# A two-layer decoder trunk on one core: layer 1's output product as seven half-size block products, with the block sums of its weight made during attention

## The chip, the core and the metric

One core of a Trainium2 chip runs the whole program. The metric is device time in microseconds (us) of one execution; of several executions the median counts. PE is the engine of the matrix products (PEld its weight loads), DVE the vector engine, ACT the scalar engine, POOL the GpSimd engine; SP only issues DMA transfers here, and ACT issues some too.

## What is computed

The reference has two layers over a sequence of 1024 rows of width 1024, all float32. Layer 0 (a recurrence and a gated spatial mix) is the same before and after. Layer 1 is sliding-window attention with a gate, then one output product:

```python
def swa_mixer(h, w_in, sinks, w_out):          # layer 1
    p = h @ w_in                               # q (16 heads of 64), k, v (2 heads each), z
    ...                                        # banded softmax, window 128, ALiBi, sinks
    y = out.reshape(bsz, t_len, ODD_MIX) * jax.nn.silu(z)
    return y @ w_out                           # 1024x1024 times 1024x1024

for i in range(DEPTH):
    ...
    x = x + gate * y                           # gate: one row of 1024, the same for every row of x
return rmsnorm(x, final_g)                     # per row: x / sqrt(mean(x*x) + eps) * final_g
```

## The kernel before

A float32 product is made of three passes of a faster format: each operand is split into `hi` (a copy that ACT rounds) and `lo` (the raw value less `hi`, by DVE, named `V` in the code, or POOL, named `G`), and `mm` on line 118 is called for hi·hi, hi·lo and lo·hi into the same PSUM tile. So every weight block passes through a tile `wraw` (three buffers, loaded by the SP queue), an ACT copy and a subtraction before PE can use it.

Layer 1 works on the transposed stream. The head pair n (two heads of 64) takes part n of w_in: `head_projs(n)` makes the queries (`qproj`) and the gate path (`zgate`, into `y`) for both halves of the sequence, 512 rows each. `attend(n, half, ...)` (lines 1187 to 1241) then goes over four blocks of 128 queries. For each: scores on PE into `pS`; DVE adds the bias (L1207); ACT takes the exponential (L1211); DVE the reciprocal (L1213); POOL scales each head's scores `Sx` (L1215); PE transposes them into `pT` (L1221); ACT and DVE split that (L1226, L1227); PE multiplies with the values into `po`. For each pair of blocks ACT and DVE add the two accumulators into `cm` (L1236 to L1239), and POOL multiplies `y` by it (L1241). `y` is then the transposed left operand of the output product, [128, 8, 1024].

Order: within layer 1 a scheduler sets the order of each engine from the program text, the dependences and priorities; `attend` stands at a raised priority. Each engine and each DMA queue takes its instructions in that order, one by one. For the head pairs 4 to 7 (N1 = 4) the second half's `attend` is written after the loop and after the loads of the output weight, so its work is mixed with that of the first output rows.

The output weight `owo` is loaded in 16 pieces of 128x512 through `wraw` (lines 1292 to 1301), split by ACT (L1299) and by DVE and POOL in turn (L1300). Then, for each of eight blocks of 128 rows (L1321 to L1354): `y` is split into `yh` (ACT, L1325) and `yl` (DVE, 128x1024, L1326); for each half of 512 columns PE makes 24 matmuls (8 blocks of the inner dimension, 3 passes) into a PSUM tile `op`; DVE multiplies it by `gate` (L1338) and adds it to the residual `xr` (L1339); ACT takes the sum of squares (L1340); DVE and POOL make the scale of the row (L1344 to L1346); DVE scales both halves (L1349); two DMAs store them. The last block is cut into columns of 512, 256 and 256, so that less is left after the last matmul. The weight is not multiplied by the gate; each product is.

Of the kernel before, what the change touches and what calls it, by code (L numbers as in the profile page):

```python
# [93 lines left out]
def tile_kernel(ctx, tc, x, cons, par, rows, ada, ada0, ew, wup, sgw, sgb, ewo, ow, owo, out, dbg=None):  # L94
# [1057 lines left out]
    at = ctx.enter_context(tc.tile_pool(name="at", bufs=1, side="right", reuse_waits="tile"))  # L1152
# [32 lines left out]
    N1 = 4  # L1185
# [64 lines left out]
    def qproj(n, w, half):  # L1250
        pt = proj(w, h, half)
        Q = []
        for e in range(2):
            a = slice(e * 64, e * 64 + 64)
            o = slice(64 - e * 64, 128 - e * 64)
            tag, bufs = ("QL", 2 * (KC - N1)) if half and n >= N1 else ("Q", 8)
            q = at.tile([P, HT], F32R, name="Q", tag=tag, bufs=bufs)
            S.activation(q[a, :], pt[a, :], AF.Copy, scale=-0.125)
            V.scalar_tensor_tensor(out=q[o, :], in0=pt[a, :], scalar=-0.125, in1=q[a, :].bitcast(F32), op0=ALU.mult, op1=ALU.subtract)
            Q.append(q)  # L1260
        qs[n, half] = Q

    def head_projs(n):
        wq = wload(ow[n])
        if n < KC - 1:
            for half in range(2):
                qproj(n, wq, half)
        wz = wload(ow[10 + n])
        for half in range(2):
            if n == KC - 1:  # L1270
                qproj(n, wq, half)
            zgate(n, wz, half)
# [9 lines left out]

    qs = {}
    head_projs(0)
    for n in range(KC):
        bias = biases(n)
        for half in range(2 if n < N1 else 1):
            with tc.high_priority(offset=BOOST):
                attend(n, half, qs[n, half], bias)
        if n + 1 < KC:  # L1290
            head_projs(n + 1)

    wo = []
    for n in range(2):
        hi, lo = new_hh(n)
        for k in range(KC):
            raw = wp.tile([P, HT], F32, name="wraw", tag="wraw", bufs=3)
            nc.sync.dma_start(out=raw, in_=owo[k * P:(k + 1) * P, n * HT:(n + 1) * HT])
            S.activation(hi[:, k, :], raw, AF.Copy)  # L1299
            (V if k % 2 else G).tensor_tensor(out=lo[:, k, :], in0=raw, in1=hi[:, k, :].bitcast(F32), op=ALU.subtract)  # L1300
        wo.append((hi, lo))
    for n in range(N1, KC):
        with tc.high_priority(offset=BOOST):
            attend(n, 1, qs[n, 1], biases(n))
    if "y1" in dbg:
        for j in range(8):
            nc.sync.dma_start(out=dbg["y1"][j], in_=y[:, j, :])


    def half_tiles(name, tag, bufs, src, dt=F32):  # L1310
        ts = [at.tile([P, HT], dt, name=name, tag=tag, bufs=bufs) for n in range(2)]
        for n in range(2):
            nc.scalar.dma_start(out=ts[n], in_=src(slice(n * HT, (n + 1) * HT)))
        return ts

    gate = half_tiles("gate", "Q", 8, lambda ns: gated[1, ns].partition_broadcast(P))
    gb = half_tiles("gateb", "zth", 2, lambda ns: rows[1, ns].partition_broadcast(P))
    for n in range(2):
        V.tensor_tensor(out=gate[n], in0=gate[n], in1=gb[n], op=ALU.add)
    fg = half_tiles("fg", "zth", 2, lambda ns: rows[2, ns].partition_broadcast(P))  # L1320
    for b in range(NB):  # L1321
        sl = slice(b * P, (b + 1) * P)
        yh = wp.tile([P, KC, P], F32R, name="yh", tag="whi", bufs=2)
        yl = wp.tile([P, KC, P], F32R, name="yl", tag="wlo", bufs=2)
        S.activation(yh, y[:, :, sl], AF.Copy)  # L1325
        V.tensor_tensor(out=yl, in0=y[:, :, sl], in1=yh.bitcast(F32), op=ALU.subtract)  # L1326
        xt = half_tiles("xr", "Q", 8, lambda ns: x1d[sl, ns])
        st = at.tile([P, 4], F32, name="st", tag="st", bufs=4)
        cuts = (0, HT, D) if b < NB - 1 else (0, HT, HT + 256, D)
        for i, (c0, c1) in enumerate(zip(cuts, cuts[1:])):  # L1330
            wh, wl = (w[:, :, c0 % HT:c0 % HT + c1 - c0] for w in wo[c0 // HT])
            xs_ = xt[c0 // HT][:, c0 % HT:c0 % HT + c1 - c0]
            pt = pproj("op")[:, 0:c1 - c0]
            for k in range(KC):
                mm(pt, lhsT=yh[:, k, :], rhs=wh[:, k, :], start=(k == 0), stop=False)
                mm(pt, lhsT=yh[:, k, :], rhs=wl[:, k, :], start=False, stop=False)
                mm(pt, lhsT=yl[:, k, :], rhs=wh[:, k, :], start=False, stop=(k == KC - 1))
            V.tensor_tensor(out=pt, in0=pt, in1=gate[c0 // HT][:, c0 % HT:c0 % HT + c1 - c0], op=ALU.mult)  # L1338
            V.tensor_tensor(out=xs_, in0=pt, in1=xs_, op=ALU.add)  # L1339
            S.activation(pt, xs_, AF.Square, accum_out=st[:, i:i + 1])  # L1340
            if b == NB - 1:
                (V if c1 == D else G).tensor_tensor(out=xs_, in0=xs_, in1=fg[c0 // HT][:, c0 % HT:c0 % HT + c1 - c0], op=ALU.mult)
        for i in range(1, len(cuts) - 1):
            V.tensor_tensor(out=st[:, 0:1], in0=st[:, 0:1], in1=st[:, i:i + 1], op=ALU.add)  # L1344
        V.tensor_scalar(out=st[:, 0:1], in0=st[:, 0:1], scalar1=1.0 / D, scalar2=NORM_EPS, op0=ALU.mult, op1=ALU.add)
        G.tensor_tensor(out=st[:, 3:4], in0=st[:, 0:1], in1=nhalf[:, 0:1], op=ALU.pow)  # L1346
        for n in range(2):
            if b < NB - 1:
# [61 lines left out]
```

## Time and profile before

| what | value |
|---|---|
| time, median of 3 runs | 1119.16 us (1118.9 to 1120.5) |
| the profiled execution: its own time, and its span in the trace | 1120.78 us, 1119.0 us |
| mean granted clock of PE, as a share of full speed | 0.976 |
| busy share of the span: PE, DVE, ACT, POOL | 93%, 64%, 47%, 34% |
| matmuls in the program | 7912 |
| layer 1's attention, roughly | from 745 us, its last pieces at 1067 us |
| output product on PE | from 1003 us on, alone from about 1050 to 1112 us |

The span is the time from the first to the last instruction of the trace; it is a little shorter than the execution's own time. A row of a timeline gives the start in us, the duration in us, the engine, the line in the kernel, the operation, and `result<-operands` with its shape; in brackets stands how long the engine sat idle before it and what ended that.

### The profile page before, as it was taken

How to read it: one execution, taken by the hardware profiler on the slowest of the kernel's cores; microseconds unless marked ns; L12 is line 12 of the kernel's file. 1: busy time of each engine (PE TensorE's matmuls, PEld its weight loads, DVE VectorE, ACT ScalarE, POOL GpSimd, SP SyncE). 2: the span in 40 equal slices, each digit the busy share in tenths (PEclk: the TensorE clock that was granted, in tenths of full speed). 3: DMA queues.
4: the chain of work that ended last, by engine and by line, in shares of the span. 5: the costliest groups of instructions: out<-in, count | busy, mean ns of one | idle time of the engine just before them, and what ended most of it. 6: DMA issues, size and time to landing. Idle time of an engine off the chain costs nothing. (4 is left out here: it accounts for less than half of the span.)

```text
span 1119.0 us, 20771 instructions
## 1 busy us (share of the span) xinstructions
PE 1038.8 (93%) x7912; PEld 833.5 (74%) x7912; DVE 716.3 (64%) x1666; ACT 526.6 (47%) x1252; POOL 382.5 (34%) x474
## 2 busy tenths in 40 slices
PE   3899898999898898989998999999999999999997
PEld 2677676677676676676776788878888888878886
DVE  6865858585749576777545367764655644478754
ACT  5575435554344436553332132234665654487521
POOL 3642405131215123233335100043554543467201
PEclk8799999999989999998999999999999999999999
DMA  8710212122202321133334244321100111152121
GB/s 306 267 26 20 78 57 67 31 67 67 76 13 68 101 66 60 39 104 105 124 118 149 90 135 134 121 71 48 39 27 31 39 39 38 52 181 67 70 95 56
DMA packets 55131, 93.42 MB, mean 83 GB/s; under 512 B 5748, under 2 KB 15988, under 8 KB 55032
## 3 DMA queue, kind: packets, MB, share of 16 engines
q1 hardware_dynamic: 45032, 77.10, 21.4%
q10 hardware_dynamic: 10000, 15.01, 4.1%
q8 instruction: 62, 1.02, 0.4%
q14 instruction: 37, 0.30, 0.1%
HBM read 79.49 MB, written 12.59 MB: 82 GB/s over the span
## 5 line engine op out<-in xcount | busy, mean ns | idle before, releaser
L118 PE MATMUL pproj<-hi,wlo 128*128 128x512 f32 x704 | 285.0, 405 | 2.4 <-POOL wlo L246 2.4
L118 PE MATMUL pproj<-hi,whi 128*128 128x512 f32 x704 | 284.7, 404 | 0.8 <-ACT vt L1175 0.7
L118 PE MATMUL pproj<-lo,whi 128*128 128x512 f32 x704 | 285.0, 405 | 0.0
L246 POOL TENSOR_TENSOR wlo<-wraw,whi 128x512 fp32r<-128x512 f32 x86 | 115.9, 1368 | 170.2 <-ACT whi L245 169.4
L118 PEld LDWEIGHTS pproj<-hi,whi 128*128 128x128 f32 x704 | 133.8, 190 | 28.8 <-issue 2.1
L118 PEld LDWEIGHTS pproj<-hi,wlo 128*128 128x128 f32 x704 | 133.4, 189 | 28.3 <-POOL wlo L246 3.3
L118 PEld LDWEIGHTS pproj<-lo,whi 128*128 128x128 f32 x704 | 133.9, 190 | 25.5 <-issue 0.5
L245 ACT ACTIVATE whi<-wraw 128x512 fp32r<-128x512 f32 x102 | 59.0, 623 | 76.8 <-PE htp L122 31.6
L118 PE MATMUL op<-wo,whi 128*128 128x512 f32 x256 | 80.8, 396 | 1.1 <-ACT whi L245 1.1
L1211 ACT ACTIVATE Sx<-Sx,nm 128x257 f32<-128x257 f32 (+1 forms) x128 | 62.3, 489 | 27.7 <-DVE nm L1207 25.8
L1207 DVE CUSTOM_DVE_ANT_0 Sx<-pS,bias,nsink 128x256 f32<-128x256 f32 (+1 forms) x128 | 53.5, 464 | 30.2 <-PE pS L118 28.9
L1215 POOL TENSOR_SCALAR Sx<-Sx,rc 128x256 f32<-128x256 f32 (+1 forms) x128 | 60.5, 487 | 26.3 <-DVE rc L1213 23.8
L842 DVE SCALAR_TENSOR_TENSOR adacc<-araw,cond,adacc 128x512 f32<-128x512 f32 x56 | 48.7, 869 | 27.5 <-DMA araw<-ada 27.3
L1227 DVE TENSOR_TENSOR PL<-pT,PH 128x512 fp32r<-128x512 f32 (+1 forms) x64 | 41.7, 655 | 30.2 <-ACT PH L1226 29.6
L118 PEld LDWEIGHTS op<-wo,whi 128*128 128x128 f32 x256 | 48.0, 188 | 12.9 <-ACT whi L245 1.5
L118 PE MATMUL op<-hi,yl 128*128 128x512 f32 (+1 forms) x136 | 51.8, 381 | 0.4 <-DVE yl L1326 0.4
L118 PE MATMUL op<-hi,yh 128*128 128x512 f32 (+1 forms) x136 | 51.7, 380 | 0.4 <-ACT yh L1325 0.4
L118 PE MATMUL op<-lo,yh 128*128 128x512 f32 (+1 forms) x136 | 51.6, 379 | 0.0
L118 PE MATMUL op<-wo,wlo 128*128 128x512 f32 x128 | 51.3, 400 | 0.0
L645 DVE TENSOR_TENSOR pr<-Lf,LT 128x2 f32<-128x2 f32 (+14 forms) x120 | 45.2, 376 | 2.6
L213 POOL TENSOR_TENSOR st<-st,nhalf 128x1 f32<-128x1 f32 x16 | 10.4, 650 | 98.8 <-DVE st L212 98.8
L1226 ACT ACTIVATE PH<-pT 128x512 fp32r<-128x512 f32 (+1 forms) x64 | 35.7, 563 | 17.8 <-PE pT L1221 16.4
(310 smaller groups left out, 2151.2 us busy)
## 6 DMA issues: line engine op xcount, KB each, us to landing
araw<-ada SPq DMA_DIRECT2D x64, 256.0 KB, 2.7
wraw<-ew SPq DMA_DIRECT2D x50, 256.0 KB, 3.0
wraw<-ow SPq DMA_DIRECT2D x36, 256.0 KB, 2.9
adaraw<-ada SPq DMA_DIRECT2D x16, 512.0 KB, 5.8
x<-x SPq DMA_DIRECT2D x8, 512.0 KB, 6.2
woraw<-ewo SPq DMA_DIRECT2D x16, 256.0 KB, 3.1
xr<-x ACTq DMA_DIRECT2D x16, 256.0 KB, 3.1
wraw<-y0d SPq DMA_DIRECT2D x16, 256.0 KB, 4.5
```

Of the source, the lines that this page charges most:

```text
L118: last[0] = nc.tensor.matmul(out, lhsT=lhsT, rhs=rhs, **kw).ins
L213: G.tensor_tensor(out=st[:, 3:4], in0=st[:, 2:3], in1=nhalf[:, 0:1], op=ALU.pow)
L245: a = S.activation(hi[:, gs, :], raws[g], AF.Copy)
L246: b = E.tensor_tensor(out=lo[:, gs, :], in0=raws[g], in1=hi[:, gs, :].bitcast(F32), op=ALU.subtract)
L645: V.tensor_tensor(out=pr[:, 0:nc_, 0:i + 1], in0=Lf[:, i:i + 1, 0:i + 1].to_broadcast([P, nc_, i + 1]), in1=LTt[:, 0:nc_, 0:i + 1], op=ALU ...
L842: op = V.scalar_tensor_tensor(out=acc, in0=raw, scalar=cond[:, k:k + 1], in1=acc, op0=ALU.mult, op1=ALU.add)
L1207: V.tensor_tensor_reduce(out=Sx[:, e, off:2 * P], in0=pS3[:, e, 0:nk], in1=bias[e][:, off:], scale=1.0, scalar=nsink[:, hd:hd + 1], op0=AL ...
L1211: S.activation(pr[:, e, off:2 * P + 1], Sx[:, e, off:2 * P + 1], AF.Exp, bias=nm[:, e:e + 1], scale=-1.0, accum_out=sm[:, e:e + 1])
L1215: G.tensor_scalar(out=pr[:, e, off:2 * P], in0=pr[:, e, off:2 * P], scalar1=rc[:, e:e + 1], scalar2=0.5, op0=ALU.mult, op1=ALU.mult)
L1226: S.activation(PH[:, ks, :], pT2[:, ks, :], AF.Copy)
L1227: V.tensor_tensor(out=PL[:, ks, :], in0=pT2[:, ks, :], in1=PH[:, ks, :].bitcast(F32), op=ALU.subtract)
```

## The change

Left operand y and weight W are each seen as 2x2 blocks of 512x512 (y's rows by its inner dimension, W's inner dimension by its columns). Eight block products make the output before; now seven do, with Winograd's form of Strassen's scheme. With B the gated weight, the seven right operands are B11, B21, B22, T1 = B12 − B11, T3 = B22 − B12, T2 = T3 + B11 and T4 = B21 − T2; the left ones are blocks of y or sums of them (`s3`, `s1`, `s2`, `s4`).

1. The gate is folded into the weight: `load_gate` (after the first head pair) makes two gate tiles, and `make_ops(k)` (after head pairs 1 to 4, one k of four each) loads four pieces of 128x512, multiplies each by the gate and makes the four sums, all on POOL: eight operations of 128x512 for each k. The seven results are written by SP to a DRAM scratch `wgd`.
2. `load_op` reads an operand back through `wraw` in four pieces and splits it (ACT, then DVE or POOL). B11 comes after head pair 5, the others during the output product.
3. No attention is held back: `attend` runs for both halves of every head pair within the loop, and the queries of the next pair are made before the gate path of this one.
4. The output product runs as B11 (four blocks of 128 rows, results kept in `t1` by ACT), T3, B21, and then for each p of four the products with T2, T1, B22 and T4. Each has 12 matmuls of 512 columns; the last T4 is made in two parts of 256.
5. DVE no longer multiplies by the gate. It adds PSUM results to the residual tiles, ten times for a pair of row blocks where there were four, since most products go into two or more places. `x_add` adds `t1` to all 16 residual tiles (12 on POOL, 4 on DVE). The sums of blocks of y and the splits of them are new work on DVE and POOL: `stemp` and `ysplit` with p = 0 on DVE and p = 1 to 3 on POOL, a part of p = 0 there too.

```diff
-    for n in range(KC):
-        bias = biases(n)
-        for half in range(2 if n < N1 else 1):
+    q_projs(0)
+    for n in range(KC):
+        if n + 1 < KC:
+            q_projs(n + 1)
+        z_projs(n)
+        bias = biases(n)
+        for half in range(2):
             with tc.high_priority(offset=BOOST):
                 attend(n, half, qs[n, half], bias)
+        if n == 0:
+            load_gate()
+        elif n < 5:
+            make_ops(n - 1)
+        elif n == 5:
+            load_op("B11", in_pre, (G,))
...
+    def make_ops(k):
...
+        def block(r, c):
+            t = pre("wg")
+            nc.sync.dma_start(out=t, in_=owo[(4 * r + k) * P:(4 * r + k + 1) * P, c * HT:(c + 1) * HT])
+            G.tensor_tensor(out=t, in0=t, in1=gate[c], op=ALU.mult)
+            return t
...
+        t = pre("wg")
+        G.tensor_tensor(out=t, in0=b12, in1=b11, op=ALU.subtract)
+        put("T1", t)
...
+    def load_op(name, tiles, E):
+        for k in range(4):
+            raw = wp.tile([P, HT], F32, name="wraw", tag="wraw", bufs=3)
+            nc.sync.dma_start(out=raw, in_=wgd[OPS.index(name), k])
+            hi, lo = tiles(k)
+            S.activation(hi, raw, AF.Copy)
+            E[k % len(E)].tensor_tensor(out=lo, in0=raw, in1=hi.bitcast(F32), op=ALU.subtract)
...
+    def ysplit(raw, E, late=False):
...
+        S.activation(t[:, 0], raw, AF.Copy)
+        E.tensor_tensor(out=t[:, 1], in0=raw, in1=t[:, 0].bitcast(F32), op=ALU.subtract)
...
+    def prod(pt, a, name, cs=slice(0, HT)):
+        for k, (wh, wl) in enumerate(W[name]):
+            mm(pt, lhsT=a[:, 0, k, :], rhs=wh[:, cs], start=k == 0, stop=False)
+            mm(pt, lhsT=a[:, 0, k, :], rhs=wl[:, cs], start=False, stop=False)
+            mm(pt, lhsT=a[:, 1, k, :], rhs=wh[:, cs], start=False, stop=k == 3)
...
+    def x_add(b, n, E):
+        nc.sync.dma_start(out=xs[b][n], in_=x1d[b * P:(b + 1) * P, n * HT:(n + 1) * HT])
+        E.tensor_tensor(out=xs[b][n], in0=xs[b][n], in1=t1[b % 4], op=ALU.add)
+
+    for b in range(4, 8):
+        x_add(b, 0, G)
+        x_add(b, 1, V)
+    load_op("T3", in_hp("hi0"), (V, G))
+    load_op("B21", in_hp("lo0"), (V, G))
...
+    for p in range(4):
+        s3 = wp.tile([P, 4, P], F32, name="sy", tag="wraw", bufs=3)
+        V.tensor_tensor(out=s3, in0=yblock(0, 0, p), in1=yblock(1, 0, p), op=ALU.subtract)
+        pt = prod(pproj("op"), ysplit(s3, V), "T3")
+        add(p + 4, 0, pt)
+        add(p + 4, 1, pt)
+    for b in range(4):
+        x_add(b, 0, G)
+    load_op("T2", in_hp("hi1"), (V,))
+    load_op("T1", in_hp("lo1"), (V,))
+    for b in range(4):
+        x_add(b, 1, G)
+    for p in range(4):
+        pt = prod(pproj("op"), ysplit(yblock(0, 1, p), V), "B21")
+        add(p, 0, pt)
+        sq(p, 0, pt)
+    load_op("B22", in_hp("B22", ot), (V, G))
+    load_op("T4", in_pre, (V, G))
...
+    for p in range(4):
+        b = p + 4
+        E = G if p else V
+        s1 = stemp(E, yblock(1, 0, p), yblock(1, 1, p), ALU.add)
+        s2 = stemp(E, s1, yblock(0, 0, p), ALU.subtract)
+        s4 = stemp(G, yblock(0, 1, p), s2, ALU.subtract)
+        a2, a1, a4, a22 = ysplit(s2, E), ysplit(s1, E), ysplit(s4, G, True), ysplit(yblock(1, 1, p), G, True)
+        pt = prod(p1("S"), a2, "T2")
+        add(b, 1, pt)
+        add(p, 1, pt)
+        add(b, 0, pt)
+        pt = prod(p1("S"), a1, "T1")
...
+        pt = prod(p1("T"), a4, "B22")
...
+            pt = prod(p1("T"), a22, "T4")
...
+        G.tensor_tensor(out=x22, in0=x22, in1=fg[1], op=ALU.mult)
+        for i in range(2):
+            cs = slice(i * 256, i * 256 + 256)
+            pt = prod(pproj("op")[:, 0:256], a22, "T4", cs)
+            V.tensor_tensor(out=x21[:, cs], in0=pt, in1=x21[:, cs], op=ALU.add)
```

What the scheduler makes of it. On DVE, before, this stands in the middle of the output rows, when no attention is left: the split of a later row block, then for each half a multiplication by the gate and an add from PSUM (`op` is a PSUM tile), then the row's scale (`xr`, `st`, `fg` are SBUF tiles).

```order
L1326 TENSOR_TENSOR yl_11365<-y1_7628,yh_11364 128x1024
L1338 TENSOR_TENSOR op_11301<-op_11301,gate_11062 128x512
L1339 TENSOR_TENSOR xr_11296<-op_11301,xr_11296 128x512
```

After, at the products with T3 and then B21 (`sy_…` are the sums s3, `ya_…` their splits or those of blocks of y, `wo_…` a part of the weight's `lo`; the lines are those of the new kernel: L1371 `ysplit`, L1414 `x_add`, L1423 the adds from PSUM, L1333 `load_op`):

```order
L1371 TENSOR_TENSOR ya_11288<-sy_11285,ya_11288 128x512
L1414 TENSOR_TENSOR xr_11140<-xr_11140,t1_11161 128x512
L1423 TENSOR_TENSOR xr_11137<-op_11267,xr_11137 128x512
L1423 TENSOR_TENSOR xr_11138<-op_11267,xr_11138 128x512
L1414 TENSOR_TENSOR xr_11142<-xr_11142,t1_11196 128x512
L1371 TENSOR_TENSOR ya_11308<-sy_11305,ya_11308 128x512
L1414 TENSOR_TENSOR xr_11144<-xr_11144,t1_11196 128x512
L1423 TENSOR_TENSOR xr_11139<-op_11287,xr_11139 128x512
L1423 TENSOR_TENSOR xr_11140<-op_11287,xr_11140 128x512
L1371 TENSOR_TENSOR ya_11328<-sy_11325,ya_11328 128x512
```

Operations on two SBUF tiles (the splits and `x_add`) now stand between the adds from PSUM, and PE's next product waits for a split that is queued behind them.

On POOL, before, the output rows hold little: the end of the attention's multiplications and one small power for each row block.

```order
L1241 TENSOR_TENSOR y1_7628<-y1_7628,cm_10851 128x256
L1241 TENSOR_TENSOR y1_7628<-y1_7628,cm_10918 128x256
L1346 TENSOR_TENSOR st_11228<-st_11228,nhalf_73 128x1
L1241 TENSOR_TENSOR y1_7628<-y1_7628,cm_10989 128x256
L1241 TENSOR_TENSOR y1_7628<-y1_7628,cm_11056 128x256
L1346 TENSOR_TENSOR st_11300<-st_11300,nhalf_73 128x1
```

After, from the end of the attention on (L1376 is `stemp`), in the products with T3 and B21:

```order
L1241 TENSOR_TENSOR y1_7628<-y1_7628,cm_11111 128x256
L1376 TENSOR_TENSOR sy_11516<-y1_7628,sy_11514 128x512
L1376 TENSOR_TENSOR sy_11606<-y1_7628 128x512
L1414 TENSOR_TENSOR xr_11137<-xr_11137,t1_11161 128x512
L1414 TENSOR_TENSOR xr_11139<-xr_11139,t1_11161 128x512
L1371 TENSOR_TENSOR ya_11524<-sy_11516,ya_11524 128x512
L1414 TENSOR_TENSOR xr_11141<-xr_11141,t1_11196 128x512
L1371 TENSOR_TENSOR ya_11527<-y1_7628,ya_11527 128x512
L1414 TENSOR_TENSOR xr_11143<-xr_11143,t1_11196 128x512
L1414 TENSOR_TENSOR xr_11129<-xr_11129,t1_11161 128x512
L1376 TENSOR_TENSOR sy_11608<-sy_11606,y1_7628 128x512
```

and seven more `x_add` follow: from `sy_11516` to the last of them 17 operations of 128x512 stand together there, without a break, each on two SBUF tiles.

168 lines of the change are left out of this document (99 added, 69 removed).

## Prediction

> **What bounds the kernel now.** I read the busy table by windows first, for layer 1 from the attention (750 us) to the end. Columns: window, length, busy us and number of instructions of each engine, granted clock, DMA share, GB/s.
>
> ```profile
> 750.00:975.00 225.00, 225.00 (x1233) 193.34 (x1232) 120.55 (x358) 125.86 (x343) 108.10 (x199) 1.00 0.12 38
> 975.00:1025.00 50.00, 47.45 (x270) 40.00 (x268) 39.00 (x114) 37.94 (x102) 33.14 (x56) 1.00 0.42 132
> 1025.00:1050.00 25.00, 25.00 (x144) 21.76 (x143) 22.62 (x59) 16.19 (x46) 12.08 (x23) 1.00 0.18 64
> 1050.00:1075.00 25.00, 25.00 (x126) 21.06 (x125) 16.29 (x27) 9.19 (x20) 3.31 (x5) 1.00 0.24 85
> 1075.00:1112.00 37.00, 36.73 (x185) 31.22 (x183) 16.87 (x30) 7.59 (x18) 3.68 (x5) 1.00 0.21 72
> 1112.00:1119.00 7.00, 0.00 (x0) 0.00 (x0) 1.76 (x6) 1.23 (x3) 0.55 (x1) 0.64 0.20 75
> ```
>
> PE is busy in all of the first 362 us but 2.8, at full clock. DVE, ACT and POOL have about half of the time free in the attention, and POOL nearly all of it in the last output rows (3.31 of 25 us). The view of waits names what PE waited for in layer 1:
>
> ```profile
> PE pS L118 <- DVE nm L1207: 0.7, 1, 0.7
> PE po L118 <- ACT PH L1226: 0.5, 1, 0.5
> PE po L118 <- DVE PL L1227: 0.5, 1, 0.5
> PE op L118 <- DVE yl L1326: 0.4, 1, 0.4
> PE op L118 <- ACT yh L1325: 0.4, 1, 0.4
> ```
>
> So PE's work is the time here, and matmuls taken away are worth their full length, as long as the other engines keep up with what they get instead. That is the question, since these engines get much.
>
> **Matmuls removed.** Two halves of the columns with 24 matmuls of 512 columns, over 8 row blocks, make 384; seven products of 4 blocks with 12 each make 336: 48 fewer. A record lasts 0.39 us, but records overlap; the pitch counts:
>
> ```profile
> 1092.67 0.39 PE L118 MATMUL op<-hi,yl 128*128 128x512 f32 x1
> 1092.90 0.39 PE L118 MATMUL op<-hi,yh 128*128 128x512 f32 x1
> 1093.13 0.39 PE L118 MATMUL op<-lo,yh 128*128 128x512 f32 x1
> ...
> 1095.14 0.70 DVE L1338 TENSOR_TENSOR op<-op,gate 128x512 f32<-128x512 f32 x1 [0.46 <-PE op L118]
> 1106.02 0.70 DVE L1338 TENSOR_TENSOR op<-op,gate 128x512 f32<-128x512 f32 x1 [0.65 <-PE op L118]
> ```
>
> From the gate multiplication of one row block to the same one of the next, 1095.14 to 1106.02, lie 48 matmuls: 10.88 us, 0.2267 each, which the starts above agree with. Saved: **−10.9 us** (48 records of 0.39 would be 18.7, which would count the overlap twice). Cutting the last T4 in two parts costs nothing: before has such a cut too.
>
> **The weight's sums.** make_ops adds on POOL 8 operations of 128x512 for each of four k, and load_gate two: 34 in all. Loads take their places on SP, 16 pieces as before, plus 28 stores and 28 loads of 256 KB; DMA share was 0.12 to 0.42 and SP waits for nobody but `wraw` buffers. The price of such an operation on POOL:
>
> ```profile
> L1300 POOL TENSOR_TENSOR lo<-wraw,hi x8: 1282/1294/1305, 982.0 to 1017.2; 128x512 fp32r<-128x512 f32 x8
> L1300 DVE TENSOR_TENSOR lo<-wraw,hi x8: 691/768/1714, 983.4 to 1016.0; 128x512 fp32r<-128x512 f32 x8
> L1339 DVE TENSOR_TENSOR xr<-op,xr x17: 425/691/692, 1014.8 to 1112.2; 128x512 f32<-128x512 f32 x15, 128x256 f32<-128x256 f32 x2
> ```
>
> 34 × 1.29 = 44 us on top of 108 in the window of 225: POOL would be busy two thirds of the time, and some 80% while the sums are made (0.48 + 41 us in about 130 us, an estimate from four of the head pairs). POOL's scale (L1215) stands in PE's way, but the transposes now stand a head's products further behind the scores than before, so I cost this at 0; its cover is that distance, and when it is used up every 1.29 us ahead of a scale goes to PE. Only the start has less cover: load_gate's add waits for a `wraw` buffer in POOL's queue with the first scales behind it. Estimate 0 to 1 us, I take **+0.5**.
>
> **No attention held back.** PE's idle 2.55 us in 975 to 1025 fall mostly to the rows above, at the place where held-back attention, weight loads and first output rows meet. After, the same meeting is at the end of attention with the B11 product as filler: between −1.8 and 0, I take **−0.5**.
>
> **The middle of the output product** decides the sign. DVE and POOL get work there on two SBUF tiles each, and in this trace such operations hold each other up:
>
> ```profile
> 982.02 2.55 POOL L1300 TENSOR_TENSOR lo<-wraw,hi 128x512 fp32r<-128x512 f32 x2 [3.41 <-ACT hi L1299]
> 983.42 1.71 DVE L1300 TENSOR_TENSOR lo<-wraw,hi 128x512 fp32r<-128x512 f32 x1
> ...
> 1001.78 1.29 POOL L1300 TENSOR_TENSOR lo<-wraw,hi 128x512 fp32r<-128x512 f32 x1
> 1002.44 1.18 DVE L1300 TENSOR_TENSOR lo<-wraw,hi 128x512 fp32r<-128x512 f32 x1
> 1003.05 0.84 POOL L1279 TENSOR_SCALAR bias<-alibi 128x256 f32<-128x256 f32 x1
> ...
> 1011.65 0.72 DVE L1300 TENSOR_TENSOR lo<-wraw,hi 128x512 fp32r<-128x512 f32 x1
> 1011.80 0.91 POOL L1215 TENSOR_SCALAR Sx<-Sx,rc 128x256 f32<-128x256 f32 x1
> 1012.29 0.21 DVE L1213 RECIPROCAL rc<-sm 128x2 f32<-128x2 f32 x2
> 1013.83 0.48 POOL L1215 TENSOR_SCALAR Sx<-Sx,rc 128x256 f32<-128x256 f32 x1
> ```
>
> DVE's split, 0.69 alone, began at 983.42 and ended at 985.13, 0.56 after POOL's second operation (984.57); the one at 1002.44 ended 0.55 after POOL's (1003.07). It waits for POOL's whole instruction. POOL's scale at 1011.80 took 0.91 under a DVE split, at 1013.83 0.48: +0.43. DVE's adds from PSUM (L1339: median 0.691, maximum 0.692) never show it. So a pair of one DVE and one POOL operation in turn takes 1.29 + 0.43 = 1.72 us.
>
> The Trainium skill, "SBUF — State Buffer", section "Who interferes with whom", says the same as a rule: a vector instruction with two SBUF inputs and a GpSimd instruction that reads SBUF exclude each other for a whole instruction, with no contention when DVE has at most one SBUF input. By a rule in which they shared the port evenly, the term below would be near zero; the rows 1.71 and 1.18 beside 0.69 go with the exclusion.
>
> In the T3 and B21 stage, up to the last split for B21, DVE has 17 operations on two SBUF tiles (4 x_adds, the splits and sums of y, splits of T2 and T1) and 10 adds from PSUM. Back to back such operations follow at 0.64 (from 1011.65 to 1012.29 above): 27 × 0.64 = 17.3 us, just inside PE's 7 products of 12 matmuls, 7 × 2.72 = 19.1 us. But POOL has 17 operations of 128x512 in a row in its queue there, which nothing but loads and `t1` gates. In turn, 17 × 1.72 = 29.2 us, and the adds from PSUM fit beside POOL's instructions. 29.2 − 19.1 = **+10.1 us**: PE waits for `lo` of each y block, and POOL's work stands in front of it. Low end 0 (POOL's 17 run out earlier or later than DVE's; alone, DVE fits), high end 17 × (0.55 + 1.29) + 10 × 0.2 − 19.1 = 14.2, when a DVE operation begins only as POOL's ends and a part of the PSUM adds stays outside.
>
> **The last stage**, from T2 on (4 × 10.9 us): POOL has for p = 1 to 3 the sums and splits, 22 operations × 1.29 = 28.4, 5 powers (0.55 each, POOL in the last row of the first fence; 2.7) and about 14 DVE operations that hold it for 0.43 each, 6.0: 37.2 us, against 34.7 of PE from its first of them to the last split needed: **+2.5**. Low end 0, high end +5 (with splits of B22 and T4, four of them POOL's, late by their loads). These loads go through three `wraw` buffers, each free again only after its split.
>
> **Tail.** After the last matmul came, in the chain of waits (start, length):
>
> ```profile
> 1110.89 0.85 PE op L118 x7
> ...
> 1111.77 0.44 DVE op L1338
> 1112.24 0.44 DVE xr L1339
> 1112.75 0.52 ACT op L1340 x2
> 1113.30 0.42 DVE xr L1342
> 1113.83 0.16 DVE st L1345
> 1114.10 0.59 POOLq L1406
> 1114.70 0.72 ACT xr L1353
> ...
> L1349 DVE SCALAR_TENSOR_TENSOR xr<-xr,st,fg x14: 734/752/1331, 1030.1 to 1104.6; 128x512 f32<-128x512 f32 x14
> ```
>
> The multiplication by the gate (0.44) goes; one more add of `st` (0.1), and on DVE two scalings of row block 3 (0.75 each) come between, of which one I take to lie on the path, and x21 is scaled whole by DVE: −0.44 + 0.1 + 0.75 + 0.2 = **+0.6**, from −0.4 to +1.4.
>
> **Sum.** −10.9 + 0.5 − 0.5 + 10.1 + 2.5 + 0.6 = +2.3. On the profiled execution's 1120.78 that is 1123.1; that execution is 1.6 above the median of the runs, so on the median 1119.16 it is **1121.5 us**. 0.2% of it, 2.2 us, is about what a measurement of this kernel can tell from no change.
>
> **Rivals.**
> (A) *The exclusion costs PE little*: POOL's x_adds come to lie where DVE only has adds from PSUM, or DVE runs ahead, and splits are ready early. For it: DVE alone fits into 17.3 of 19.1 us, and POOL's first x_adds wait for `t1` and loads. Against: both queues are filled from the same moment on, the end of attention, and DVE has 2 us to spare only. With 0 to 5 in place of 12.6: 1109 to 1114, middle 1111. Decides if DVE's splits in that stage average under 0.9 us.
> (B) *The weight's way through DRAM is late*: each operand is four loads one behind the other through three buffers, and in the last stage T2, T1, B22 and T4 follow closely. For it: SP's queue has loads of `xr` and `fg` between, and a buffer is released only by a split that itself waits for POOL. Against: the DMA share. Four loads late by 1.5 us more each: 1127 to 1134. It decides if PE waits for `wraw` splits of L1333 in sum over 5 us.
> (C) *POOL is late in attention*: if two thirds busy is too much where the queue holds 8 sums ahead of a scale, 1 to 2 us for each of four head pairs: 1116 with (A), 1127 with the rest. Against: 33 of 50 us busy with only 2.6 of PE idle, in 975 to 1025.
>
> **Chances.** Forecast case (PE loses 7 to 15 us in the output product: 1116 to 1125) 0.57; A 0.25; B 0.10; C 0.08. Faster by over 0.2% is below 1117: A, 0.04 of the forecast case and half of C, 0.33. Between 1117 and 1121.4: 0.23 of the forecast case and a little of C, 0.25. Above: 0.42. The range goes down to A's lower part, 1110, and up to where B begins, 1127.5; the forecast case's own range is 1116 to 1125.
>
> **What would show it.** In the trace after: attention with PE at 100% (C fails); 336 times 0.2267 us of output matmuls; in T3 and B21, splits of y and x_adds on DVE with a mean of 1.1 to 1.7 us instead of 0.69, POOL busy over 90%, and PE waiting for DVE `ya` for some 10 us; in the last stage, PE waiting for POOL `ya` for 2 to 3 us; a tail of 7.9 us from the last matmul where it was 7.3. I am wrong if those splits take 0.7 and PE is gapless (A), or if its waits name the weight's splits (B).

## The result, and the profile after

The changed kernel takes 1127.54 us (median of 6 runs, 1125.4 to 1133.06) against 1120.33 for the kernel before (6 runs, 1118.9 to 1122.92): ratio 1.0067, 95% interval 1.0045 to 1.0088. It is slower by 5 to 10 us. The forecast was 1121.5 us, 2.3 above the kernel before. It had the sign right, with a chance of only 0.42 on a time above 1121.4, and the size too small: the measured median lies 0.04 us above its range of 1110 to 1127.5.

The profiled execution took 1133.06 us, 5.5 above the median, with a span of 1131.3. Windows of layer 1 after, cut at the first T3 matmul, the first T2 matmul and the last matmul (same columns as before):

```profile
752.30:1038.30 286.00, 285.09 (x1609) 246.60 (x1610) 178.50 (x526) 182.71 (x493) 196.30 (x318) 1.00 0.28 88
1038.30:1070.50 32.20, 25.85 (x98) 18.45 (x97) 31.55 (x31) 12.06 (x23) 24.38 (x16) 0.95 0.44 133
1070.50:1119.30 48.80, 46.55 (x205) 35.63 (x203) 40.23 (x56) 20.42 (x46) 36.05 (x29) 1.00 0.29 97
1119.30:1131.30 12.00, 0.00 (x0) 0.00 (x0) 6.88 (x14) 2.38 (x8) 3.38 (x5) 0.60 0.36 131
```

The attention with POOL's sums in it (first row) leaves PE almost no gap (285.09 of 286.00 us busy). In the second row, T3 and B21, DVE is busy for 31.55 of 32.20 us: PE's eight products need 21.8 us (96 × 0.2267), DVE is now the bound. The third row needs 43.5 us of matmuls and takes 48.8. The tail, where before had 7.3 us, has 12.0. PE's busy time (25.85 in the second row) is more than 21.8, since records last longer than the pitch; a stage's loss is read from its length against the pitch, not from PE's idle time.

What PE waited for in layer 1 (in all, times, longest):

```profile
PE op L118 <- DVE ya L1371: 5.1, 4, 2.5
PE htp L122 <- DVE xr L1042: 1.9, 1, 1.9
PE pS L118 <- POOL ya L1371: 1.4, 1, 1.4
PE op L118 <- DVE xr L1423: 1.0, 2, 0.5
```

The first, third and fourth are the output product's; the second lies at the end of layer 0, in code that the change does not touch.

Groups of operations from 1030 us to the end (count | busy us, mean ns | idle before), DVE first, and from 750 us for POOL:

```profile
L1401 DVE SCALAR_TENSOR_TENSOR xr<-xr,st,fg 128x512 f32<-128x512 f32 x14 | 16.6, 1225 | 2.0 <-POOL st L1396 1.9
L1423 DVE TENSOR_TENSOR xr<-pS,xr 128x512 f32<-128x512 f32 x20 | 12.6, 677 | 0.0
L1371 DVE TENSOR_TENSOR ya<-sy,ya 128x512 fp32r<-128x512 f32 x6 | 7.7, 1290 | 0.9 <-ACT ya L1370 0.9
L1414 DVE TENSOR_TENSOR xr<-xr,t 128x512 f32<-128x512 f32 x4 | 7.0, 1756 | 0.0
...
L1414 POOL TENSOR_TENSOR xr<-xr,t 128x512 f32<-128x512 f32 x12 | 19.1, 1620 | 0.0
```

Operations of one shape and one engine: with an operand in PSUM (L1423, `pS`) 0.68 us, with both in SBUF 1.2 to 1.76 on average in these groups. The timeline shows the two queues in turn, DVE's three rows and then POOL's:

```profile
1045.96 1.70 DVE L1414 TENSOR_TENSOR xr<-xr,t 128x512 f32<-128x512 f32 x1
1047.58 1.74 DVE L1371 TENSOR_TENSOR ya<-sy,ya 128x512 fp32r<-128x512 f32 x1
1049.25 1.77 DVE L1414 TENSOR_TENSOR xr<-xr,t 128x512 f32<-128x512 f32 x1
...
1047.07 3.40 POOL L1414 TENSOR_TENSOR xr<-xr,t 128x512 f32<-128x512 f32 x2
1050.43 1.73 POOL L1376 TENSOR_TENSOR sy<-sy,y 128x512 f32<-128x512 f32 x1
```

One of each in 1.67 us (1047.58 to 1049.25): the pair that the prediction put at 1.72. The pairs were fewer than forecast, though. DVE has the 17 operations on two SBUF tiles that the prediction counted (4 `x_add`s, 8 splits and sums of y, 5 splits of T2 and T1), from 1037.97 to 1067.7 us, but only the first twelve took 1.67 to 1.83 us. POOL did its 17 faster than DVE, because it went on while DVE did the adds from PSUM; its last `x_add` ended at 1062.7, and DVE's next five took 0.67 to 0.74 us each. Three rows at that point (POOL's seven last `x_add`s, then DVE's last slow and first quick operation):

```profile
1052.12 10.56 POOL L1414 TENSOR_TENSOR xr<-xr,t 128x512 f32<-128x512 f32 x7
1061.46 1.76 DVE L1333 TENSOR_TENSOR wo<-wraw,wo 128x512 fp32r<-128x512 f32 x1
1063.75 0.67 DVE L1371 TENSOR_TENSOR ya<-y,ya 128x512 fp32r<-128x512 f32 x1
```

Where layer 1 begins, and why (ACT's first copy of v before and after; then, after, SP's queue and DVE's two scalings of the last row block of layer 0):

```profile
744.90 0.60 ACT L1175 ACTIVATE vt<-pproj 128x512 f32<-128x512 f32 x1 [0.63 <-PE pproj L118]
752.33 0.60 ACT L1176 ACTIVATE vt<-pproj 128x512 f32<-128x512 f32 x1 [1.04 <-PE pproj L118]
...
738.39 0.86 SPq L1293 DMA_DIRECT2D gate<-gated  x2
739.30 0.90 SPq L1305 DMA_DIRECT2D wg<-owo  x2
740.30 0.38 SPq L1039 DMA_DIRECT2D x1d<-xr  x1
742.37 0.48 DVE L1042 TENSOR_SCALAR xr<-xr,st 128x512 f32<-128x512 f32 x1 [0.73 <-POOL st L213]
746.74 0.48 DVE L1042 TENSOR_SCALAR xr<-xr,st 128x512 f32<-128x512 f32 x1 [3.88 <-DMA x1d<-xr]
```

Four new loads (two of the gate, two of the output weight) went ahead of the last store of `x1`. DVE scales that tile in place: it had to wait 3.88 us, until 6.4 us after the store's issue, and PE 1.9. The other 5.5 us of layer 0 belong to this execution: from 425 to 450 us it was granted a clock of 0.80, where the execution before had 1.00:

```profile
425.00:450.00 25.00, 22.00 (x321) 17.93 (x321) 14.29 (x27) 13.49 (x31) 7.39 (x7) 0.80 0.10 34
425.00:450.00 25.00, 22.06 (x295) 18.06 (x288) 14.80 (x27) 14.57 (x34) 9.78 (x8) 1.00 0.21 63
```

(after, then before). These 5.5 us are about what the profiled execution lies above the median, and no term below explains them. The profiles of the experiments say the same: layer 1 begins at 743.1 to 745.9 us in the kernel before and in the five kernels without loads ahead of that store, at 747.3 to 750.5 in the six others that have them, and at 752.3 only here.

### The profile page after: what moved, and what is told of

It reads as the page before. It is cut to its first block, busy times and chain, and to the rows that moved or that the text cites. A ratio compares the mean times of both kernels' runs of the same rounds, so it can differ in the third digit from the quotient of the medians.

```text
span 1131.3 us, 20946 instructions
## 1 busy us (share of the span) xinstructions
PE 1037.6 (92%) x7852; PEld 826.8 (73%) x7852; DVE 754.4 (67%) x1693; ACT 545.5 (48%) x1288; POOL 479.3 (42%) x542
## 5 line engine op out<-in xcount | busy, mean ns | idle before, releaser
L1215 POOL TENSOR_SCALAR Sx<-Sx,rc 128x256 f32<-128x256 f32 (+1 forms) x128 | 57.8, 466 | 22.4 <-DVE rc L1213 22.0
L213 POOL TENSOR_TENSOR st<-st,nhalf 128x1 f32<-128x1 f32 x16 | 10.4, 651 | 99.2 <-DVE st L212 99.2
L1221 PE MATMUL pT<-con,Sx 128*128 128x128 f32 x240 | 38.4, 272 | 0.0
L1258 DVE SCALAR_TENSOR_TENSOR Q<-pproj,Q 64x512 fp32r<-64x512 f32 x32 | 22.0, 689 | 19.5 <-ACT Q L1257 19.1
L118 PE MATMUL pS<-KH,Q 128*128 128x256 f32 (+1 forms) x128 | 34.0, 287 | 0.0
```

The lines of the kernel that those rows point to most:

```text
L118: last[0] = nc.tensor.matmul(out, lhsT=lhsT, rhs=rhs, **kw).ins
L1215: G.tensor_scalar(out=pr[:, e, off:2 * P], in0=pr[:, e, off:2 * P], scalar1=rc[:, e:e + 1], scalar2=0.5, op0=ALU.mult, op1=ALU.mult)
L1221: nc.tensor.transpose(pT4[:, kb, e, :], pr[:, e, kb * P:(kb + 1) * P], ident)
```

## The experiments

Eleven kernels ran. Each was timed beside the kernel before on the same chip, so ratios to it are what compares: that of the changed kernel is 1.0067. Two of them leave work out: "POOL memset" (12 of the 16 residual tiles get neither `x` nor `t1`) and "scaling on ACT" (12 of the 16 output tiles lack final_g). In the others the outputs are complete.

| kernel | base | time, us | ratio to before | interval |
|---|---|---|---|---|
| none held back | before | 1127.41 | 1.0064 | 1.0046 to 1.0083 |
| four loads | before | 1122.86 | 1.0025 | 1.0009 to 1.0040 |
| new order of projections | before | 1123.19 | 1.0012 | 0.9992 to 1.0032 |
| POOL memset | changed | 1118.98 | 0.9988 | 0.9970 to 1.0006 |
| scaling on ACT | changed | 1123.15 | 1.0028 | 1.0013 to 1.0044 |
| raw in PSUM | changed | 1116.20 | 0.9967 | 0.9953 to 0.9981 |
| final_g in PSUM | changed | 1121.88 | 1.0013 | 0.9993 to 1.0033 |
| loads later | changed | 1124.24 | 1.0039 | 1.0025 to 1.0054 |
| old order of projections | changed | 1131.13 | 1.0090 | 1.0067 to 1.0112 |
| three mends | changed | 1110.71 | 0.9922 | 0.9902 to 0.9942 |
| three mends, t1 in PSUM | changed | 1108.31 | 0.9882 | 0.9859 to 0.9905 |

**Is it the reads?** POOL's `x_add`s are replaced by instructions that keep POOL busy and read nothing.

```diff
-        E.tensor_tensor(out=xs[b][n], in0=xs[b][n], in1=t1[b % 4], op=ALU.add)
+        if E is V:
+            V.tensor_tensor(out=xs[b][n], in0=xs[b][n], in1=t1[b % 4], op=ALU.add)
+        else:
+            for _ in range(3):
+                G.memset(xs[b][n], 0.0)
```

> The changed kernel with the twelve x_adds of POOL replaced by three memsets each of the same residual tile (those residual tiles lose x and t1). POOL is about as long busy (12 x some 1.4 us) at the same places, but these instructions read nothing. Theory (exclusion over SBUF reads): DVE's splits and x_adds beside them go back to 0.7 us from 1.7, and the T3 and B21 stage loses 2 to 5 us instead of 12; the time is 1117 to 1121 us against 1127.5. Rival 1 (POOL is late, so that PE and DVE wait for its results): the stage still loses over 10 us and the time stays within 2 us of 1127.5. Rival 2 (the weight's way through DRAM sets the stage): the same, with PE waiting for wo of L1333.

1118.98 us, ratio 0.9988: 8 to 9 us less than the changed kernel. Groups of that kernel (DVE, then POOL), and what PE waited for most:

```profile
L1333 DVE TENSOR_TENSOR wo<-wraw,wo 128x512 fp32r<-128x512 f32 x10 | 6.8, 686 | 0.2 <-ACT wo L1332 0.2
L1371 DVE TENSOR_TENSOR ya<-y,ya 128x512 fp32r<-128x512 f32 x5 | 3.4, 682 | 0.0
L1371 DVE TENSOR_TENSOR ya<-sy,ya 128x512 fp32r<-128x512 f32 x6 | 7.1, 1186 | 1.2 <-ACT ya L1370 1.2
L1415 DVE TENSOR_TENSOR xr<-xr,t 128x512 f32<-128x512 f32 x4 | 3.7, 954 | 0.0
L1418 POOL MEMSET xr<- 128x512 f32 x36 | 17.0, 522 | 0.0
...
PE op L118 <- DVE xr L1427: 4.4, 1, 4.4
```

POOL was busy with the memsets for 17.0 us, where 12 × 1.29 would be 15.5, and DVE's splits beside them are at 0.68 again. The splits of the sums (`ya<-sy`, 1.19) and the `x_add`s (0.95) stay slower where POOL's own sums and splits of y still stand beside them. POOL is busy there about as long (24.5 us from its first sum to the last memset, 26.6 after), and the weight still comes through DRAM, so neither POOL's amount of work nor that way is what the 8 to 9 us came from.

The stage itself gained less than expected. Up to the end of its 96 matmuls it still lost about 7 us (1036.0 to 1065.1, with one T2 matmul in between), where 2 to 5 were forecast; 4.4 of them are the one wait above. The edit moved the scheduler's order too: DVE's first add from PSUM (1044.58) stands behind all four `x_add`s and the T3 splits here, and PE waits for it. The time came out as forecast because the last stage lost less as well (about 0.6 us where after lost 5.3). So this kernel shows what reads cost an operation, and the next one what that costs the stage.

**The same with the operand moved.** Nothing is left out here and DVE has no operation less; ACT has 16 copies more.

```diff
         S.activation(t[:, 0], raw, AF.Copy)
+        if stage:
+            staged = p1(stage).rearrange("p (k q) -> p k q", k=4)
+            S.activation(staged, raw, AF.Copy)
+            raw = staged
         E.tensor_tensor(out=t[:, 1], in0=raw, in1=t[:, 0].bitcast(F32), op=ALU.subtract)
...
-    load_op("T2", in_hp("hi1"), (V,))
-    load_op("T1", in_hp("lo1"), (V,))
+    load_op("T2", in_hp("hi1"), (V,), "S")
+    load_op("T1", in_hp("lo1"), (V,), "S")
```

(`load_op` the same way; the splits for T3 and B21 with stage="T".)

> The changed kernel; in the stage of the T3 and B21 products ACT copies the raw operand of DVE's splits (of y, T2 and T1) to PSUM first, so that these 16 operations have one operand in PSUM and one in SBUF. Nothing is left out; POOL's x_adds stay where they are. Theory (exclusion between DVE operations on two SBUF tiles and POOL): those splits take 0.65 to 0.7 us instead of 1.7, and only the four x_adds and the sums on DVE are still held up; the stage loses 3 to 6 us instead of 12, and the time is 1119 to 1122 us against 1127.5. Rival (DVE's and ACT's order or the weight's way through DRAM holds PE up): ACT's 16 copies more of 0.6 us make the splits later still, and the time is 1127 us or more.

1116.20 us, ratio 0.9967, faster than the kernel before, and by more than expected. Groups:

```profile
L1337 DVE TENSOR_TENSOR wo<-pS,wo 128x512 fp32r<-128x512 f32 x8 | 5.5, 689 | 2.4 <-ACT pS L1335 2.4
L1379 DVE TENSOR_TENSOR ya<-pT,ya 128x512 fp32r<-128x512 f32 x8 | 5.5, 684 | 0.4 <-ACT ya L1374 0.4
L1422 DVE TENSOR_TENSOR xr<-xr,t 128x512 f32<-128x512 f32 x4 | 4.8, 1198 | 0.0
L1422 POOL TENSOR_TENSOR xr<-xr,t 128x512 f32<-128x512 f32 x12 | 16.6, 1422 | 0.0
```

All 16 splits take 0.69 us beside the same POOL queue. From the first T3 to the first T2 matmul it is 24.3 us (1033.7 to 1058.0) instead of 32.2, a loss of 2.5 us instead of 10.4, with DVE's and POOL's order nearly as after. The last stage gained too: 46.2 (to 1104.2) instead of 48.8; POOL came to its sums earlier there, which may be why.

**The last stage and the tail.** Twelve of DVE's 14 scalings go to ACT, without final_g:

```diff
-            V.scalar_tensor_tensor(out=xt[n], in0=xt[n], scalar=sts[b][:, 3:4], in1=fg[n], op0=ALU.mult, op1=ALU.mult)
+            if b in (3, 7):
+                V.scalar_tensor_tensor(out=xt[n], in0=xt[n], scalar=sts[b][:, 3:4], in1=fg[n], op0=ALU.mult, op1=ALU.mult)
+            else:
+                S.activation(xt[n], xt[n], AF.Copy, scale=sts[b][:, 3:4])
```

> The changed kernel with the final scaling of the row blocks 0 to 2 and 4 to 6 on ACT, by the row's factor alone (final_g is left out for these rows): 12 operations with two SBUF inputs go from DVE. Theory: in the last stage they hold DVE up (1.2 us each beside POOL) and POOL's sums behind them, so that DVE is 4 to 5 us late after the last matmul; then the time from the last matmul to the end falls from 12.0 us to 7.5 to 9, the last stage loses under 2 us instead of 3, and the time is 1121 to 1124 us against 1127.5. Rival: the tail is long because of its own work (adds, scaling of block 3 and POOL's multiplication of x22): 11 us or more, and 1126 to 1128 us.

1123.15 us, 4 us under the changed kernel; from the last matmul to the end 8.7 us (1112.3 to 1121.0) instead of 12.0. The last stage gained little: 48.0 us (1064.3 to 1112.3), a loss of 4.5 where under 2 was expected. What the tail gained may be the scalings' length or the exclusion; so the scalings were then left on DVE and only final_g was moved, by two copies of ACT to PSUM:

```diff
+    fgp = [ps.tile([P, HT], F32, name="fgp", tag="O", bufs=2) for n in range(2)]
+    for n in range(2):
+        S.activation(fgp[n], fg[n], AF.Copy)
...
-            V.scalar_tensor_tensor(out=xt[n], in0=xt[n], scalar=sts[b][:, 3:4], in1=fg[n], op0=ALU.mult, op1=ALU.mult)
+            V.scalar_tensor_tensor(out=xt[n], in0=xt[n], scalar=sts[b][:, 3:4], in1=fgp[n], op0=ALU.mult, op1=ALU.mult)
```

> The changed kernel with final_g copied once to two PSUM tiles, from which DVE's 14 scalings read it. Nothing is left out, and DVE has as many operations as before. Theory: the scalings take 0.7 us instead of 1.23, POOL's sums and splits beside them 1.29 instead of up to 1.75; the tail after the last matmul falls from 12.0 us to 8 to 10, the time to 1123 to 1125.5 us. With the scalings moved to ACT the kernel took 1123.15; what this one takes above that is their own length on DVE, and not the exclusion. Rival: the whole 4.4 us there were DVE's length; then 1126 to 1128 us here.

1121.88 us, ratio 1.0013, as good as with the scalings off DVE.

```profile
L1401 DVE SCALAR_TENSOR_TENSOR xr<-xr,st,fgp 128x512 f32<-128x512 f32 x14 | 9.7, 742 | 1.3 <-POOL st L1396 1.3
```

The 14 scalings took 9.7 us in place of 16.6, the last stage 45.3 us (1066.1 to 1111.4) instead of 48.8, the tail 8.8; the time is below the 1123 to 1125.5 that was expected. DVE does as many operations as after, so the exclusion was the cost, and not the work. That taking the scalings off DVE left the last stage at 48.0 is not explained; ACT has twelve operations more there.

**The loads ahead of the store.** First added to the kernel before, whose order on PE does not change by it:

```diff
     qs = {}
+    for i in range(4):
+        d = y[:, 7 - i // 2, i % 2 * HT:(i % 2 + 1) * HT]
+        nc.sync.dma_start(out=d, in_=gated[1, i * HT:(i + 1) * HT].partition_broadcast(P) if i < 2 else owo[0:P, i % 2 * HT:(i % 2 + 1) * HT])
     head_projs(0)
```

> The kernel before with four loads of 256 KB (two of the gate's row to all partitions, two of the output weight) put on SP's queue ahead of the last store of x1, where the changed kernel has its gate and weight loads; they go into parts of y that are written over later, and nobody reads them. PE's order is that of before. Theory: the last store of x1 lands some 4 us later behind these loads, DVE's second scaling of that row block (L1042) waits for it, and PE loses 1.9 us: 1121.5 to 1122.5 us against 1120. Rival: the loads are off the path and the 1.9 us of the profiled execution are chance; then no wait for xr L1042 on PE and no difference (within 1 us).

1122.86 us, ratio 1.0025 (1.0009 to 1.0040): slower by 1 to 4.5 us. The waits of PE and the second scaling of DVE:

```profile
PE htp L122 <- DVE xr L1042: 2.0, 1, 2.0
740.52 0.49 DVE L1042 TENSOR_SCALAR xr<-xr,st 128x512 f32<-128x512 f32 x1 [4.01 <-DMA x1d<-xr]
```

The same wait, where the kernel before has none. Then they were held back in the changed kernel, with a small copy from a tile that arrives later, so that the store goes first:

```diff
             g = pre("gate")
+            G.tensor_copy(g[:, 0:16], nsink)
             nc.sync.dma_start(out=g, in_=gated[1, ns].partition_broadcast(P))
...
             t = pre("wg")
+            if k == 0:
+                G.tensor_copy(t[:, 0:16], nsink)
             nc.sync.dma_start(out=t, in_=owo[(4 * r + k) * P:(4 * r + k + 1) * P, c * HT:(c + 1) * HT])
```

> The changed kernel with the gate's and the first two weight loads held until the sinks have arrived (a copy of 128x16 from them into each of the four tiles ahead of its load), so that on SP's queue the last store of x1 comes before them. The scheduler's order in attention moves with it. Theory: PE no longer waits for xr L1042, layer 1 begins 2 to 3 us earlier, and the time is 1124.5 to 1126 us against 1127.5. Rival: the sums come later, and POOL, which is 98% busy from 780 to 860 us, then holds the attention up: PE waits for Sx L1215, and no gain (1127 us or more).

1124.24 us, ratio 1.0039: 2.8 × 10⁻³ or 3 us less than the changed kernel, with layer 1 starting at 744.43 us. Its intervals and those of the changed kernel overlap, but the wait is gone from the trace. The scheduler gave the attention another order with it, so that the gain is not purely the store's.

**The attention.** From layer 1's start to the last matmul the two profiled executions differ by nothing (366.8 and 367.0 us), although the losses above outweigh the matmuls. Before the first T3 matmul something was gained: 286.0 us after, B11 in it; before, 366.8 less eight row blocks of 10.88 (87.0) plus B11's 10.9 makes 290.7. In the other changed kernels that stretch took 285.6 to 288.7 us, so that the gain is 2 to 5 us, and 4.7 in this pair. Three kernels asked for its cause. First nothing held back, in the kernel before:

```diff
-    N1 = 4
+    N1 = 8
```

> The kernel before with N1 = 8: no attention held back, nothing else. In the pair of profiles the stretch from layer 1's first copy of v to the last matmul, less 88 (before) and 77 us of output matmuls (after), is some 4 to 5 us shorter after. Theory: that came from holding nothing back; then this kernel takes 1114 to 1117 us against 1120 of before, and PE has under 1 us of idle time from 790 us to the last matmul. Rival: it came from the B11 product and the new order of the projections; then this one takes 1119 us or more, since without the held-back attention PE has nothing to do while the output weight's splits are finished (1 to 6 us of waits for L1300).

1127.41 us, 7 us slower, as the rival said. PE's waits:

```profile
PE pT L1221 <- POOL Sx L1215: 2.5, 2, 1.3
PE po L118 <- ACT PH L1226: 1.8, 2, 1.6
PE op L118 <- ACT yh L1325: 1.8, 1, 1.8
```

PE has nothing to do between the last blocks' steps, and then waits for the first split of `y`. Holding attention back is worth 7 us to the kernel before. Then the new order of projections alone, in the kernel before, and the old one in the changed kernel:

```diff
-        if n + 1 < KC:
-            head_projs(n + 1)
+        if n + 1 < KC:
+            q_projs(n + 1)
+        z_projs(n)
```

> The kernel before with the changed kernel's order of projections (the queries of the next head pair ahead of the gate path of this one), attention of the second halves still held back. From layer 1's first copy of v to the first T3 matmul the changed kernel takes 286.0 us, B11 in it; the kernel before takes 279.8 us for the same without B11's 10.9, so 4.7 were gained somewhere. Theory: by the order of projections, with which a score's way through DVE, ACT and POOL has more matmuls beside it: 1116 to 1118 us against 1120. Rival: by B11's matmuls in the attention's last part, in place of a load of the output weight; then no gain here (1119 to 1123 us).

> The changed kernel with the order of projections of before (queries and gate path of a head pair one behind the other, ahead of its attention), all else as changed. Theory (order of projections): the attention with POOL's sums in it loses what the order gained and more, 4 to 8 us: 1131 to 1136 us against 1127.5, with waits of PE for Sx L1215. Rival (the B11 product as filler): within 2 us of 1127.5.

In the kernel before the new order gains nothing (1.0012, 0.9992 to 1.0032). In the changed kernel the old order costs about 2.5 us (1.0090 against 1.0067, intervals that overlap), but not in the attention: from layer 1's start to the first T3 matmul it is 286.2 us there, as after, and not the 4 to 8 us more that were expected. It loses in the next stage, with one wait of 10.5 us of PE for an add to `xr` (L1423). So the order of projections did not make the 4.7 us. What is left is B11's products in place of held-back attention as work beside the last head pairs, and the loads of the output weight that no longer stand there: in the waits of before about 2.5 us lie at that place. That is argued and not tried by itself, and the rest stays open.

**All mends together.** The two moves to PSUM and the later loads in one kernel, then also `t1` for DVE's four `x_add`s by a copy of ACT to PSUM:

> The three edits together (raw operands in PSUM, final_g in PSUM, loads later), nothing left out. If each is worth what the theory says and they add up: 1127.5 - 7 - 3 - 2 = 1115 to 1116 us, faster than before (1120.5) by 0.3 to 0.5%. If the losses hide behind one another (the stages have one bound each, so that a mended one uncovers the next): 1118 to 1122 us, no clear difference from before.

> The kernel with the three edits (1110.7 us), and DVE's four x_adds also read t1 from PSUM, where ACT copies it; nothing left out. These four took 1.2 us each beside POOL, and POOL's x_adds 1.42. Theory: both go to 0.7 and 1.29, the T3 and B21 stage (25.0 us, 21.8 of matmuls) loses 1 to 2 us less: 1108.5 to 1110.5 us. Rival: PE's waits there (wo L1340, 1.4 us) are now those of the weight's way, and nothing changes (within 1 us).

```diff
+        t = t1[b % 4]
+        if E is V:
+            t = ps.tile([P, HT], F32, name="t1p", tag="O", bufs=2)
+            S.activation(t, t1[b % 4], AF.Copy)
-        E.tensor_tensor(out=xs[b][n], in0=xs[b][n], in1=t1[b % 4], op=ALU.add)
+        E.tensor_tensor(out=xs[b][n], in0=t, in1=xs[b][n], op=ALU.add)
```

1110.71 us (0.9922) and 1108.31 us (0.9882, 0.9859 to 0.9905): both faster than the kernel before, the second by 11 to 16 us. The first is also below both forecasts, since the raw operands in PSUM were worth 11 us and not 7. The parts are 11, 6 and 3 us below the changed kernel each (0.0100, 0.0054 and 0.0028 of 1120), 20 in sum, and 16 together (0.0145): equal within their intervals, so that it stays open whether one hides behind another. The last edit alone is not clear of the noise, as the two intervals overlap. Windows of the last kernel, cut as those of after:

```profile
744.60:1030.20 285.60, 284.70 (x1608) 246.25 (x1609) 177.41 (x526) 184.17 (x497) 195.47 (x323) 1.00 0.28 92
1030.20:1053.90 23.70, 22.46 (x98) 17.78 (x97) 19.98 (x32) 20.83 (x41) 22.17 (x18) 1.00 0.62 197
1053.90:1098.20 44.30, 44.30 (x205) 36.62 (x204) 36.18 (x61) 21.86 (x50) 33.95 (x31) 1.00 0.33 114
1098.20:1106.10 7.90, 0.04 (x1) 0.00 (x0) 2.97 (x8) 1.23 (x3) 1.73 (x3) 0.79 0.36 133
```

PE is the bound again: 23.7 us for 21.8 of matmuls, 44.3 for 43.5, and a tail of 7.9, which is what the prediction had for it. POOL is nearly as busy as after in the last stages (22.17 and 33.95 us), DVE is not (19.98 of 23.7).

## Why the prediction was right or wrong, point by point

The terms in us, as forecast and as the two profiled executions show them:

| step of the prediction | forecast | bounds | shown |
|---|---|---|---|
| matmuls removed, by the pitch | −10.9 | | −10.9 (by their count) |
| loads on SP's queue | 0 | none given | +1.9 |
| load_gate at the start of attention | +0.5 | 0 to 1 | 0 (no such wait of PE; in the next row) |
| no attention held back | −0.5 | −1.8 to 0 | −4.7 (whole stretch to T3) |
| T3 and B21 | +10.1 | 0 to 14.2 | +10.4 (32.2 − 21.8) |
| last stage | +2.5 | 0 to 5 | +5.3 (48.8 − 43.5) |
| tail | +0.6 | −0.4 to 1.4 | +4.7 (12.0 − 7.3) |
| sum | +2.3 | | +6.7; the medians differ by 7.2 |

- **Right: the exclusion and its place; its size partly by luck.** The pair of 1.72 us came out as 1.67 to 1.7, and moving the splits' operand to PSUM took the stage's loss from 10.4 to 2.5 us. The forecast of 10.1 was 17 pairs of 1.72, with the adds from PSUM beside POOL's instructions at no cost. The trace has twelve slow operations, not 17, and the ten adds came between them at 0.6 us each; some 5 us too much and 6 too little cancel. POOL was busy for 24.38 us of the first 24.7 and then stopped, which is 76% of the stage and not over 90; PE waited 5.1 us for `ya`, not 10. The 10.4 is also one execution's: in three kernels that leave this stage as it is (final_g in PSUM, loads later, scaling on ACT) it took 29.5 to 31.0 us and lost 7.7 to 9.2. Rivals A (1109 to 1114) and B (PE waiting for weight splits) did not come; C did not either: while POOL was 98% busy, from 780 to 860 us, PE had no gap.
- **Wrong: the tail**, the largest miss. The step that failed is that DVE would be up to date when the last matmul ends. The prediction has only "two scalings of row block 3 (0.75 each)" there, "of which one I take to lie on the path", and that came true: they are DVE's last pair, and 0.75 us of it lies on the chain of waits. But the two scalings of the row block before them, by their order that of block 6, were still to come when the last matmul ended at 1119.3; they took 2.40 us, and row block 3's add of B22 (1121.89) and the last product's adds stood behind them:

```profile
1117.97 0.60 DVE xr L1423
1118.91 0.56 POOL st L1396
1119.49 2.40 DVE xr L1401 x2
1121.89 0.61 DVE xr L1423
...
1125.30 0.75 DVE xr L1401
```

  The price of 0.75 is the median of a kernel in which POOL was nearly idle in that part. All 14 scalings read two SBUF tiles, so the rule that the prediction applied to the splits holds for them as well. POOL makes the factor that a pair waits for and goes straight on to its next operation, so a pair tends to run beside one: the pairs took 1.41 to 3.48 us, 1.225 an operation on average. Of the 4.7 us, 2.6 are this late begin; the rest lies in the work behind that add. With final_g in PSUM block 6's pair took 1.40 us and had ended (1110.97) before the last matmul did (1111.4), and the tail was 8.8.
- **Wrong: the last stage**, by the same omission as far as is shown. "about 14 DVE operations that hold it for 0.43 each" counted what DVE does to POOL and not what POOL does to DVE: 14 × (1.225 − 0.742) = 6.8 us more on DVE. With final_g in PSUM the stage lost 1.8 us instead of 5.3. PE's wait for POOL's splits, the term that was forecast at 2 to 3 us, was 1.4. Which part of the rest each wait makes is open: with the scalings on ACT the stage still lost 4.5.
- **Wrong: the loads.** "SP waits for nobody but `wraw` buffers" looked at who waits on the queue, and not at what is queued behind the new loads: the store of `x1`, for which DVE waits in place. The same four loads in the kernel before made PE wait 2.0 us, where it does not wait without them.
- **Wrong in the other direction: the attention**, better by some 4 us than taken in this pair, which is luck for the sum: it hid most of the tail's miss. The prediction named holding nothing back, with B11 as the filler. Holding nothing back costs 7 us without B11, so the gain can only come from the filler or from what left that place; which, is not shown.
- The Trainium skill, "SBUF — State Buffer", section "Who interferes with whom", also says that an instruction of GpSimd that only writes does not contend with a DVE instruction that reads two SBUF inputs. The trace agrees: beside memsets DVE's splits took 0.68 to 0.69 us, beside adds up to 1.8 (in the changed kernel).

## What to carry to other kernels

When work is spread over DVE and POOL to clear PE's path, count pairs and not shares: here every DVE operation on two SBUF tiles beside a full POOL queue took some 1.7 us instead of 0.69, and the old ones of the stage, the scalings, paid as well as the new. An operand that ACT copies to PSUM first takes the operation out of this at the price of a 0.6 us copy on an engine with time to spare; here that, with the later loads, turned a loss of 0.7% into a gain of 1.2%. For each load that a change adds, look at which store or load stands behind it in its queue and who waits for that, even where this lies in code that the change leaves alone.

## What the runs showed of the hardware that was not expected

- With both queues full, POOL and DVE each got one instruction in turn (1.67 to 1.7 us a pair, where POOL's takes 1.29 alone); DVE's adds from PSUM ran at 0.68 us in between, and POOL went on beside them. This held from 1038 to 1062 us in the changed kernel.
- A store of 256 KB that was issued behind four loads of the same size let DVE go on only 6.4 us after its issue (6.6 in the kernel before with the four loads); without them the same store landed in 2.0.
- The granted clock was 0.63 and then 0.75 from 1049.4 to 1055.0 us, after a wait of PE of 2.49 us; with final_g in PSUM it stayed at 1.00 after a wait just as long. It does not order the stage's time: 30.0 us there at 1.00, 29.5 and 31.0 at 0.94 (loads later, scaling on ACT). DVE was busy for nearly all of the stage in each of them. Why the clock fell in some executions is open.
